# Two attention heads at a time in a one-layer hybrid decoder with a mixture of experts

## The chip, the cores and the metric

The kernel runs on one core of a Trainium2 chip. The metric is the device time of one execution in microseconds; a lower time is better. The core has engines that work side by side, each with its own in-order queue: PE (matrix multiply; PEld is its weight load), DVE (elementwise work on vectors), ACT (functions of one argument, from tables), and SP, which here only issues transfers. PSUM is the small memory that PE writes and DVE and ACT read, in eight banks of 512 float32 columns for each of 128 partitions.

## What is computed

One layer of a decoder trunk for 256 tokens of 1024 channels in float32. A vector c gives six adaLN vectors (shift, scale, gate, twice). Three causal branches (forgetting attention A, stick-breaking attention B, with 8 heads of 64 each, and a gated linear recurrence C) are projected, gated, summed and projected again; a top-4-of-32 mixture of experts follows.

```python
def token_mixer(h, ...):
    z = h @ w_in
    qa, ka, va, fa, qb, kb, vb, xc, gc = jnp.split(z, IN_SPLITS, axis=-1)
    logf = jax.nn.log_sigmoid(fa + b_f)
    o_a = fox_attention(fox_h(qa), fox_h(ka), fox_h(va), logf)
    o_b = stick_breaking_attention(sb_h(qb), sb_h(kb), sb_h(vb))
    o_c = rg_lru_branch(xc, gc, conv_w, conv_b, lru_wa, lru_ba, lru_wx, lru_bx, lru_lambda)
    g = jax.nn.sigmoid(h @ w_gate + b_gate).reshape(b, s, N_BRANCHES, d)
    merged = g[:, :, 0] * (o_a @ w_pa) + g[:, :, 1] * (o_b @ w_pb) + g[:, :, 2] * (o_c @ w_pc)
    return merged @ w_o
...
# fox_attention:   s = q k * scale + F_q - F_k, masked;  p = softmax(s);  out = p @ v
# stick-breaking:  log_keep = log_sigmoid(-z) below the diagonal;  cs = cumsum(log_keep)
#                  w = exp(log_sigmoid(z) + min(cs[-1] - cs, 0));  out = w @ v
# rg_lru:          a = exp(log_a);  u = sqrt(-expm1(2 * log_a)) * (i_gate * x)
#                  h_t = a_t * h_(t-1) + u_t;  out = h * gelu(gc)
...
ada = cond @ w_ada + b_ada            # shift1, scale1, gate1, shift2, scale2, gate2
y = token_mixer(x * (1 + scale1) + shift1, ...)
x = layer_norm(ALPHA * x + (1 + gate1) * y)
y = moe_ffn(x * (1 + scale2) + shift2, ...)
x = layer_norm(ALPHA * x + (1 + gate2) * y)
```

## The kernel before, in words

**Projections.** Weights arrive in pieces of 1 MB ([128, 2048] float32) in a ring of five buffers (`load`, L74). `split` (L90) makes a high part on ACT (L96) and a low part on DVE (L97) into one of three weight buffers; a projection is the sum of three products, 48 matmuls of 256 columns for each piece (`proj_T`, L278). Results go to PSUM tag `g`, two banks, and from there through ACT or DVE.

**Order.** The program is written in one order, and a planner then orders each engine's queue by the written order and by what it holds to be ready, so projections fill PE's queue between steps of the attention. The written order is: q, k, v of branch A in six projections (`qkv`), with the forget gates (`forget`), pairs 0 and 1 of the heads after three of them and pairs 2 and 3 after six; the same for branch B; four convolution projections (`conv`); the recurrence's gates, its roots (`Sqrt`, L521) and scans (L525); `w_pa`; the recurrence's other input `gl` (L548 to L552); gelu (L557), product (L558) and split of the recurrence's output; the first branch's gates (`gate_pair`, L569); then, for the second and third branch, gates and projections (`add_branch`, L583); then `w_o` in eight units with the routing (`unit`, `route`).

**Heads.** `fox` (L348) and `stick` (L437) take one head: scores on half of PE's rows into one bank of PSUM tag `a` (two banks), steps on DVE and ACT in one half of the SBUF tiles `da` and `db`, then transposes or a running sum into one bank of tag `b` (two banks). `attend` (L375) multiplies by the values, on half of PE's columns, into a bank `o` that the two heads of a pair share; L430 and L471 read it.

**Tables.** ACT holds one set of functions at a time. Order edges (`after`, L69: order only, no wait) keep the root behind the recurrence's exponentials (`end_exp`), the gelu and all gates' `Tanh` behind the roots (`end_sqrt`).

**The adaLN vectors.** Vectors 0 and 1 come first, on PE. The other four are summed by DVE while other work runs: `ada_rest` (L255) is a generator, and `ada_step` (L271), called after each projection, takes its next step where the string `ADA` has a 1. A vector has four loads of 1 MB, each with two multiply-adds over 1024 columns (L173, L175), and a fifth step that sums over partitions on PE and adds the bias. Before, vector 5 is summed at steps 4 to 8, vector 4 at 18 to 23, vector 3 at 24 to 29, vector 2 at 31 to 36; steps 1 to 12 are the attention's projections, 13 to 16 the convolution, 17 and 18 `w_pa`, 19 to 22 `gl`, 23 to 26 the first gates, 27 to 40 the other two branches.

**Experts.** The second part streams 2 MB chunks through eight places (`place_of`, L753) in the order `ROUND`. The places lie over memory of the first part: place 0 over the pool `low`, 1 to 3 over the ring and two slots of `mid`, 4 over the rest of `mid`, 5 to 7 over the weight buffers. So the first chunks, which SP issues in order, wait until those buffers are free.

Of the kernel before, what the change touches and what calls it, by code (L numbers as in the profile page):

```python
# [26 lines left out]
GSLOT = 6  # L27
# [3 lines left out]
ADA = "00001" "1" "111000" "0000" "00" "1111" "0111" "01110111" "1111111111"  # L31
WFAT = 1
ROUND = (0, 1, 3, 2, 5, 7, 4, 6)
# [15 lines left out]
def hybrid_layer_kernel(ctx: ExitStack, tc: tile.TileContext, a: dict, dbg=None):  # L49
# [66 lines left out]
    bank = banks(ps1, {"g": 2, "a": 2, "b": 2, "m": 2})  # L116
# [65 lines left out]
    xT = [bank("ab"[b // 2], f"xT{b}") for b in range(4)]  # L182
# [165 lines left out]
    def fox(h, qa, ka):  # L348
        hs = slice(64 * (h % 2), 64 * (h % 2) + 64)
        ft = h // 2  # L350
        p = bank("a", "fs")
        nf = negid[hs, h:h + 1].to_broadcast([64, 128])
        mm(p[:, :128], qa[hs, ft, :128], ka[hs, ft, :128], True, False)
        mm(p[:, :128], nf, FS[hs, :128], False, True)
        mm(p[:, 128:384], qa[hs, ft, 128:], ka[hs, ft, :], True, False)
        mm(p[:, 128:384], nf, FS[hs, :], False, True)
        s = da[:, h % 2, :384]
        V.scalar_tensor_tensor(s[:, :128], p[:, :128], Fq[:, 0, h:h + 1], fmask[:, 128:], op0=OP.add, op1=OP.add)
        V.scalar_tensor_tensor(s[:, 128:384], p[:, 128:384], Fq[:, 1, h:h + 1], fmask, op0=OP.add, op1=OP.add)
        st = m1.tile([128, 8], F32, tag="st", name="st", bufs=4)  # L360
        V.reduce_max(st[:, 0:1], s[:, :128], axis=AX.X, negate=True)
        V.reduce_max(st[:, 1:2], s[:, 128:384], axis=AX.X, negate=True)
        S.activation(s[:, :128], s[:, :128], AF.Exp, bias=st[:, 0:1], accum_out=st[:, 2:3])
        S.activation(s[:, 128:384], s[:, 128:384], AF.Exp, bias=st[:, 1:2], accum_out=st[:, 3:4])
        V.reciprocal(st[:, 4:6], st[:, 2:4])
        V.tensor_scalar(s[:, :128], s[:, :128], st[:, 4:5], None, op0=OP.mult)
        V.tensor_scalar(s[:, 128:384], s[:, 128:384], st[:, 5:6], None, op0=OP.mult)
        pt = bank("b", "fpt")
        for j in range(3):
            PE.transpose(pt[:, j * 128:(j + 1) * 128], s[:, j * 128:(j + 1) * 128], ident)  # L370
        w = db[:, h % 2, :384]
        S.activation(w, pt[:, :384], AF.Copy)
        return w

    def attend(h, w, v, o):  # L375

        hs = slice(64 * (h % 2), 64 * (h % 2) + 64)
        c = slice(64 * h, 64 * h + 64)
        mm(o[hs, :T], v[:, 0, c], w[:, :256], True, False)
        mm(o[hs, 128:T], v[:, 1, c], w[:, 256:384], False, True)  # L380
# [39 lines left out]
    for i, done in enumerate(qkv(0, "a", (2, 3, 4), ada_step)):  # L420
        if i == WFAT:
            FS, Fq, negid = forget()
        if done is None:
            continue
        qa, ka, va = done
        for hp in (2 * (i // 3), 2 * (i // 3) + 1):
            o = bank("m", "oa")
            for h in (2 * hp, 2 * hp + 1):
                attend(h, fox(h, qa, ka), va, o)
            S.activation(oah[:, hp, :], o[:, :T], AF.Copy)  # L430
            V.tensor_tensor(oal[:, hp, :], o[:, :T], oah[:, hp, :].bitcast(F32), op=OP.subtract)
# [5 lines left out]
    def stick(h, qb, kb):  # L437
        hs = slice(64 * (h % 2), 64 * (h % 2) + 64)
        ft = h // 2
        p = bank("a", "bs")  # L440
        mm(p[:, :256], kb[hs, ft, :128], qb[hs, ft, :], True, True)
        mm(p[:, 256:384], kb[hs, ft, 128:], qb[hs, ft, 128:], True, True)
        n = slice(0, 384)
        l = da[:, h % 2, n]
        S.activation(l, p[:, n], AF.Abs)
        S.activation(l, l, AF.Exp, scale=-1.0)
        S.activation(l, l, AF.Ln, bias=1.0)
        k = db[:, h % 2, n]
        V.scalar_tensor_tensor(k, p[:, n], 0.0, l, op0=OP.max, op1=OP.add)
        V.scalar_tensor_tensor(l, p[:, n], 0.0, l, op0=OP.min, op1=OP.subtract)  # L450
        for d in (0, 256):
            V.tensor_tensor(k[:, d:d + 128], k[:, d:d + 128], SU, op=OP.mult)
        q = bank("b", "bc")
        mm(q[:, n], SL, k, True, False)
        mm(q[:, 128:256], ones, k[:, 256:384], False, True)
        V.scalar_tensor_tensor(l, q[:, n], 0.0, l, op0=OP.max, op1=OP.subtract)
        i = S.activation(l, l, AF.Exp, scale=-1.0)
        for d in (0, 256):
            V.tensor_tensor(l[:, d:d + 128], l[:, d:d + 128], SU, op=OP.mult)
        return l, i  # L460

    for i, done in enumerate(qkv(6, "b", (7, 8, 9), ada_step)):
        if done is None:
            continue
        qb, kb, vb = done
        for hp in (2 * (i // 3), 2 * (i // 3) + 1):
            o = bank("m", "ob")
            for h in (2 * hp, 2 * hp + 1):
                w, last = stick(h, qb, kb)
                attend(h, w, vb, o)  # L470
            S.activation(obh[:, hp, :], o[:, :T], AF.Copy)  # L471
            V.tensor_tensor(obl[:, hp, :], o[:, :T], obh[:, hp, :].bitcast(F32), op=OP.subtract)
# [29 lines left out]
    for q in range(2):  # L502
        r, i, th = (f4(s, n) for s, n in zip(((7, 8, 9), (0, 1, 17))[q], ("r", "i", "th")))
        lru.append((r, i, th))
        for u in range(2):
            pr, pi = bank("a", "pr"), bank("b", "pi")
# [10 lines left out]
    for q, (r, i, th) in enumerate(lru):  # L517

        S.activation(xv[q], r, AF.Square)
        V.scalar_tensor_tensor(th, xv[q], 1.0, th, op0=OP.add, op1=OP.mult)  # L520
        end_sqrt = after(S.activation(th, th, AF.Sqrt, scale=0.25), end_exp)  # L521
        V.tensor_tensor(i, i, th, op=OP.mult)
        for f in range(4):
            c = slice(f * T, f * T + T)
            V.tensor_tensor_scan(th[:, c], r[:, c], i[:, c], 0.0, OP.mult, OP.add)  # L525

# [28 lines left out]
    oc = []  # L555
# [9 lines left out]
    tgu = f4(18, "tgu").rearrange("p (b c) -> p b c", b=2)  # L565

    last_tanh = [None]

    def gate_pair(b, i, out):  # L569

        p = proj_pair(a["w_gate"][4 * b + i])
        for f in range(2):
            c = 8 * b + 2 * i + f
            last_tanh[0] = after(S.activation(out[:, f, :], p[:, f * T:(f + 1) * T], AF.Tanh, scale=0.5,
                                              bias=hbg[:, c:c + 1]), end_sqrt)
        ada_step()

    for i in range(4):
        t = tgu[:, i % 2].rearrange("p (f t) -> p f t", f=2)
        gate_pair(0, i, t)  # L580
        V.scalar_tensor_tensor(merged(2 * i), t, 1.0, merged(2 * i), op0=OP.add, op1=OP.mult)

# [84 lines left out]
    def unit(t, j):  # L667
# [14 lines left out]
        pT = bank("a", "pT")  # L682
# [5 lines left out]
    def route(t):  # L688
        pl = bank("b", "pl")
# [569 lines left out]
```

## Time and profile before

| | us |
|---|---|
| median of 3 runs | 1318.84 (1317.68 to 1322.93) |
| profiled execution | 1319.59 |
| its span, first to last instruction | 1317.7 |
| PE busy | 1204.5 (91%) |
| DVE busy | 493.3 (37%) |
| ACT busy | 283.6 (22%) |

The mean granted clock of PE is 0.982 of full speed. Busy shares are means over stages with different limits, so the stages are read apart: the first part, up to about 376 us, has many small steps on four engines; the second, to about 1280 us, is the stream of expert weights; the last 38 us are the final norm. Ends of matmuls are modelled and rows of matmuls overlap, so a rate is best read from starts.

### The profile page before, as it was taken

How to read it: one execution, taken by the hardware profiler on the slowest of the kernel's cores; microseconds unless marked ns; L12 is line 12 of the kernel's file. 1: busy time of each engine (PE TensorE's matmuls, PEld its weight loads, DVE VectorE, ACT ScalarE, POOL GpSimd, SP SyncE). 2: the span in 40 equal slices, each digit the busy share in tenths (PEclk: the TensorE clock that was granted, in tenths of full speed). 3: DMA queues.
4: the chain of work that ended last, by engine and by line, in shares of the span. 5: the costliest groups of instructions: out<-in, count | busy, mean ns of one | idle time of the engine just before them, and what ended most of it. 6: DMA issues, size and time to landing. Idle time of an engine off the chain costs nothing. (4 is left out here: it accounts for less than half of the span.)

```text
span 1317.7 us, 15781 instructions
## 1 busy us (share of the span) xinstructions
PE 1204.5 (91%) x6508; PEld 616.8 (47%) x6508; DVE 493.3 (37%) x1018; ACT 283.6 (22%) x554; POOL 0.2 (0%) x4
## 2 busy tenths in 40 slices
PE   5899999999889999999999889979898988989895
PEld 2888899999843343433343233223223322323221
DVE  1765688977732431313122212212221221212224
ACT  1454559434220110200011010001101100101010
POOL 0000000000000000000000000000000000000000
PEclk9899999999989999999999999999999999999998
DMA  9854356794879999999999999999999999999991
GB/s 387 319 205 160 104 191 234 293 364 178 336 294 429 423 420 428 429 427 427 427 427 428 429 427 428 427 428 427 429 426 428 428 426 428 427 427 427 428 414 75
DMA packets 42771, 482.95 MB, mean 367 GB/s; under 512 B 4740, under 2 KB 5508, under 8 KB 9672
## 3 DMA queue, kind: packets, MB, share of 16 engines
q1 hardware_dynamic: 42024, 480.51, 88.1%
q10 hardware_dynamic: 672, 1.39, 0.3%
q8 instruction: 53, 0.87, 0.3%
q14 instruction: 22, 0.18, 0.0%
HBM read 480.83 MB, written 1.05 MB: 366 GB/s over the span
## 5 line engine op out<-in xcount | busy, mean ns | idle before, releaser
L64 PE MATMUL gu<-raw,xg 128*64 128x512 f32 x2048 | 460.7, 596 | 47.0 <-DMA raw<-in_w_gu_dram 46.7
L64 PEld LDWEIGHTS gu<-raw,xg 128*64 128x64 f32 x2048 | 140.0, 137 | 352.8 <-issue 264.4
L64 PE MATMUL yp<-raw,act 128*64 128x512 f32 x992 | 230.0, 605 | 6.2 <-DMA raw<-in_w_down_dram 3.7
L871 DVE TENSOR_TENSOR t<-pT,bge 128x256 f32<-128x256 f32 x128 | 48.4, 419 | 392.9 <-PE pT L865 391.6
L855 ACT ACTIVATE gs<-gu 128x512 f32<-128x512 f32 x64 | 38.1, 597 | 639.4 <-PE gu L64 593.9
L64 PE MATMUL pp<-hh,w 128*128 128x256 f32 x896 | 130.6, 291 | 4.7 <-ACT hh L104 4.7
L64 PEld LDWEIGHTS yp<-raw,act 128*64 128x64 f32 x992 | 67.7, 138 | 139.8 <-issue 123.8
L64 PEld LDWEIGHTS pp<-hh,w 128*128 128x128 f32 x896 | 116.7, 194 | 8.8 <-ACT hh L104 4.8
L97 DVE TENSOR_TENSOR w<-raw,w 128x2048 fp32r<-128x2048 f32 x44 | 100.6, 2287 | 34.6 <-ACT w L96 34.5
L96 ACT ACTIVATE w<-raw 128x2048 fp32r<-128x2048 f32 x44 | 84.0, 1911 | 28.3 <-PE pm L64 12.8
L939 DVE TENSOR_TENSOR x<-x,pC 128x512 f32<-128x512 f32 x60 | 38.7, 684 | 119.3 <-PE pC L64 119.3
L64 PE MATMUL pC<-y,G 64*128 64x512 f32 x248 | 68.0, 622 | 6.8 <-DVE y L894 6.4
L894 DVE TENSOR_TENSOR y<-yp,g2c 128x512 f32<-128x512 f32 x31 | 21.4, 691 | 136.6 <-PE yp L64 136.6
L64 PE MATMUL pp<-hl,w 128*128 128x256 f32 x448 | 66.2, 287 | 0.0
L64 PEld LDWEIGHTS pp<-hl,w 128*128 128x128 f32 x448 | 59.0, 193 | 1.0 <-issue 0.7
L874 ACT ACTIVATE sg<-t 128x256 f32<-128x256 f32 x64 | 26.7, 417 | 98.5 <-DVE t L872 98.5
L64 PEld LDWEIGHTS pC<-y,G 64*128 64x128 f32 x248 | 23.1, 185 | 49.0 <-issue 33.0
L865 PE MATMUL pT<-cst,gs 128*128 128x128 f32 x256 | 41.1, 286 | 4.5 <-ACT gs L855 3.7
L865 PEld LDWEIGHTS pT<-cst,gs 128*128 128x128 f32 x256 | 26.9, 140 | 38.8 <-ACT gs L855 30.4
L818 ACT ACTIVATE xg<-pgx 128x128 f32<-128x128 f32 x128 | 28.5, 275 | 55.7 <-PE pgx L64 54.9
L175 DVE SCALAR_TENSOR_TENSOR acc<-raw,cond,acc 128x1024 f32<-128x1024 f32 x28 | 35.9, 1281 | 3.2 <-DMA raw<-in_w_ada_dram 3.0
L64 PE MATMUL pgx<-P,h2h 128*128 128x256 f32 x128 | 31.2, 326 | 3.1 <-ACT G L834 0.9
(278 smaller groups left out, 897.5 us busy)
## 6 DMA issues: line engine op xcount, KB each, us to landing
raw<-in_w_gu_dram SPq DMA_DIRECT2D x128, 2048.0 KB, 32.7
raw<-in_w_down_dram SPq DMA_DIRECT2D x62, 2048.0 KB, 32.3
raw<-in_w_ada_dram SPq DMA_DIRECT2D x24, 1024.0 KB, 7.3
raw<-in_w_in_dram SPq DMA_DIRECT2D x20, 1024.0 KB, 7.0
raw<-in_w_gate_dram SPq DMA_DIRECT2D x12, 1024.0 KB, 7.2
raw<-in_w_pc_dram SPq DMA_DIRECT2D x4, 1024.0 KB, 8.6
raw<-in_w_o_dram SPq DMA_DIRECT2D x4, 1024.0 KB, 4.9
rawl<-in_w_down_dram SPq DMA_DIRECT2D x3, 1024.0 KB, 32.1
```

The costliest lines, as they stand in the source:

```text
L64: PE.matmul(out, lhsT, rhs, start=start, stop=stop)
L96: i = S.activation(wh[:, c], r, AF.Copy)
L97: j = V.tensor_tensor(wl[:, c], r, wh[:, c].bitcast(F32), op=OP.subtract)
L175: V.scalar_tensor_tensor(acc, raw[:, i, :], cond[:, k:k + 1], acc, op0=OP.mult, op1=OP.add)
L818: S.activation(x[:, k].rearrange("p e s -> p (e s)"), p[:, i * 2 * CAP:(i + 1) * 2 * CAP], AF.Copy)
L855: S.activation(gs[n], gu[n], AF.Copy)
L865: PE.transpose(p[:, f * 128:(f + 1) * 128], gs[n][:, f * 128:(f + 1) * 128], ident)
L871: V.tensor_tensor(t[:, i], pv[:, i], b[:, :, None].to_broadcast([128, 4, CAP]), op=OP.add)
L874: S.activation(sg, t[:, 0], AF.Sigmoid, scale=1.702)
L894: V.tensor_tensor(y, yp, g2c, op=OP.mult)
L939: V.tensor_tensor(acc[t][:, c], acc[t][:, c], p[n], op=OP.add)
```

## The change

`fox`, `stick` and `attend` take a pair of heads (`hp`). PSUM tags `a` and `b` become one tile of two banks each (`wide`), one bank for each head; steps that are alike for both heads become one instruction over both banks or over both halves of `da` and `db`, and matmuls of the two heads are written alternately. The recurrence's gate tiles `pr`, `pi` and three other users of the tags take such a tile too. The block with the recurrence's roots and scans moves behind the first branch's four gates, whose `Tanh` is now ordered behind `end_exp` alone; the roots are ordered behind the last of these, the other gates behind the gelu. `ADA` now has vector 5 at steps 4 to 8, vector 4 at 9 to 13, vector 3 at 27 to 31, vector 2 at 32 to 37; vector 4's accumulator is slot 14 instead of 6. `ROUND` swaps places 1 and 2.

```diff
-GSLOT = 6
+GSLOT = 14
...
-ADA = "00001" "1" "111000" "0000" "00" "1111" "0111" "01110111" "1111111111"
+ADA = "0000" "1111111111" "0000000000000" "11111111111111111"
...
-ROUND = (0, 1, 3, 2, 5, 7, 4, 6)
+ROUND = (0, 2, 3, 1, 5, 7, 4, 6)
...
-    bank = banks(ps1, {"g": 2, "a": 2, "b": 2, "m": 2})
+    bank = banks(ps1, {"g": 2, "m": 2})
+    def wide(tag, name):
+        return ps1.tile([128, 2, 512], F32, tag=tag, name=name)
...
+    HALF = slice(0, 64), slice(64, 128)
+    def fox(hp, qa, ka):
+        p = wide("a", "fs")
+        for c, q in ((slice(0, 128), slice(0, 128)), (slice(128, 384), slice(128, 256))):
+            k = slice(0, c.stop - c.start)
+            for i, hs in enumerate(HALF):
+                mm(p[:, i, c], qa[hs, hp, q], ka[hs, hp, k], True, False)
+            for i, hs in enumerate(HALF):
+                mm(p[:, i, c], negid[hs, 2 * hp + i:2 * hp + i + 1].to_broadcast([64, 128]), FS[hs, k], False, True)
+        s = da[:, :, :384]
...
+        for t, c in ((0, slice(0, 128)), (1, slice(128, 384))):
+            V.reduce_max(st[:, 0, 2 * t:2 * t + 2], s[:, :, c], axis=AX.X, negate=True)
...
+        pt = wide("b", "fpt")
+        for i in range(2):
+            for j in range(3):
+                PE.transpose(pt[:, i, j * 128:(j + 1) * 128], s[:, i, j * 128:(j + 1) * 128], ident)
+        w = db[:, :, :384]
+        S.activation(w, pt[:, :, :384], AF.Copy)
         return w
...
+    def attend(hp, w, v, o):
+        for t, oc, wc in ((0, slice(0, T), slice(0, 256)), (1, slice(128, T), slice(256, 384))):
+            for i, hs in enumerate(HALF):
+                c = slice(64 * (2 * hp + i), 64 * (2 * hp + i) + 64)
+                mm(o[hs, oc], v[:, t, c], w[:, i, wc], t == 0, t == 1)
...
-            for h in (2 * hp, 2 * hp + 1):
-                attend(h, fox(h, qa, ka), va, o)
+            attend(hp, fox(hp, qa, ka), va, o)
...
+    def stick(hp, qb, kb):
+        p = wide("a", "bs")
+        for c, k, q in ((slice(0, 256), slice(0, 128), slice(0, 256)),
+                        (slice(256, 384), slice(128, 256), slice(128, 256))):
+            for i, hs in enumerate(HALF):
+                mm(p[:, i, c], kb[hs, hp, k], qb[hs, hp, q], True, True)
+        p = p[:, :, n]
+        l, k = da[:, :, n], db[:, :, n]
+        S.activation(l, p, AF.Abs)
...
+        V.scalar_tensor_tensor(k, p, 0.0, l, op0=OP.max, op1=OP.add)
+        V.scalar_tensor_tensor(l, p, 0.0, l, op0=OP.min, op1=OP.subtract)
...
+        q = wide("b", "bc")
+        for i in range(2):
+            mm(q[:, i, n], SL, k[:, i, :], True, False)
+            mm(q[:, i, 128:256], ones, k[:, i, 256:384], False, True)
...
+        prw, piw = wide("a", "pr"), wide("b", "pi")
         for u in range(2):
-            pr, pi = bank("a", "pr"), bank("b", "pi")
+            pr, pi = prw[:, u, :], piw[:, u, :]
...
+    behind = [end_exp]
+    def gate_pair(b, i, out):
...
+                                              bias=hbg[:, c:c + 1]), behind[0])
...
+    for i in range(4):
+        t = tgu[:, i % 2].rearrange("p (f t) -> p f t", f=2)
+        gate_pair(0, i, t)
+        V.scalar_tensor_tensor(merged(2 * i), t, 1.0, merged(2 * i), op0=OP.add, op1=OP.mult)
+    for q, (r, i, th) in enumerate(lru):
+        after(S.activation(xv[q], r, AF.Square), end_exp)
+        V.scalar_tensor_tensor(th, xv[q], 1.0, th, op0=OP.add, op1=OP.mult)
+        end_sqrt = after(S.activation(th, th, AF.Sqrt, scale=0.25), last_tanh[0])
+        V.tensor_tensor(i, i, th, op=OP.mult)
+        for f in range(4):
+            c = slice(f * T, f * T + T)
+            V.tensor_tensor_scan(th[:, c], r[:, c], i[:, c], 0.0, OP.mult, OP.add)
...
-        after(S.activation(gl[q], gl[q], AF.Gelu_apprx_tanh), end_sqrt)
+        behind[0] = after(S.activation(gl[q], gl[q], AF.Gelu_apprx_tanh), end_sqrt)
```

## Rows read from the trace of the kernel before

**Rows 1.** Page, 40 slices: tenths of the time that DMA engines moved data.
```profile
DMA  9854356794879999999999999999999999999991
```

**Rows 2.** Stages: length, busy us of PE, PEld, DVE, ACT, POOL; clock, DMA share, GB/s.
```profile
110.00:190.00 80.00, 80.00 (x575) 71.02 (x574) 55.45 (x98) 42.32 (x63) 0.00 (x0) 1.00 0.41 144
190.00:243.00 53.00, 53.00 (x413) 50.71 (x412) 48.26 (x53) 41.67 (x58) 0.00 (x0) 1.00 0.65 230
243.00:294.20 51.20, 51.20 (x409) 49.28 (x409) 43.85 (x38) 19.81 (x20) 0.00 (x0) 1.00 0.95 369
294.20:333.00 38.80, 37.88 (x314) 37.36 (x313) 26.95 (x25) 19.26 (x18) 0.00 (x0) 1.00 0.46 167
376.00:1280.00 904.00, 834.08 (x3832) 293.36 (x3832) 213.94 (x569) 100.04 (x275) 0.00 (x0) 1.00 1.00 424
```

**Rows 3.** PE's timeline: start us, busy us, line, operation, out<-in, shape, count.
```profile
72.92 0.34 PE L64 MATMUL fs<-FS,negid 64*128 64x128 f32 x2
...
73.79 1.10 PE L64 MATMUL pp<-hh,w 128*128 128x256 f32 x7
...
105.31 2.08 PE L64 MATMUL pt<-w,hh 128*128 128x256 f32 x16
107.23 1.12 PE L64 MATMUL pt<-w,hl 128*128 128x256 f32 x8
108.28 0.88 PE L64 MATMUL oa<-d,va 128*64 128x256 f32 x8
109.09 1.21 PE L64 MATMUL pt<-w,hh 128*128 128x256 f32 x8
110.23 0.93 PE L64 MATMUL bs<-qTb,kTb 64*128 64x256 f32 x8
111.09 0.86 PE L64 MATMUL pp<-hh,w 128*128 128x256 f32 x5
...
115.29 0.86 PE L64 MATMUL oa<-d,va 128*64 128x256 f32 x4
...
120.75 0.92 PE L64 MATMUL bs<-qTb,kTb 64*128 64x256 f32 x4
```

**Rows 4.** PE's waits for other engines, 38 to 358 us: total us, times, longest.
```profile
PE pp L64 <- ACT hh L104: 4.7, 1, 4.7
PE py L64 <- ACT mh L104: 0.9, 1, 0.9
```

**Rows 5.** Stages by tile, PE first: `fs`, then `oa`, `bs`, `ob`.
```profile
50.00:212.00 162.00, 7.17 (x48) 4.92 (x48) 5.99 (x16) 1.00 0.54 192
50.00:212.00 162.00, 6.06 (x32) 3.30 (x32) 1.67 (x4) 1.53 (x4) 1.00 0.54 192
50.00:212.00 162.00, 6.43 (x32) 4.72 (x32) 8.73 (x16) 3.97 (x8) 1.00 0.54 192
50.00:212.00 162.00, 5.43 (x32) 2.79 (x32) 1.67 (x4) 1.52 (x4) 1.00 0.54 192
```

**Rows 6.** DVE, groups by line, 40 to 380 us: count, busy us, mean ns, idle.
```profile
L175 DVE SCALAR_TENSOR_TENSOR acc<-raw,cond,acc 128x1024 f32<-128x1024 f32 x28 | 35.9, 1281 | 3.2 <-DMA raw<-in_w_ada_dram 3.0
...
L525 DVE TENSOR_TENSOR_SCAN th<-r,i 128x256 f32<-128x256 f32 x8 | 4.9, 670 | 0.0
...
L522 DVE TENSOR_TENSOR i<-i,th 128x1024 f32<-128x1024 f32 x2 | 2.4, 1216 | 0.0
```

**Rows 7.** ACT's timeline, the table for the roots and the two gelus.
```profile
214.72 1.28 ACT L521 ACT_TABLE_LOAD   x1
...
222.08 2.00 ACT L557 ACTIVATE gl<-gl 128x1024 f32<-128x1024 f32 x2
```

**Rows 8.** SP's timeline: transfers of the first expert chunks, issue times.
```profile
311.54 56.74 SPq L759 DMA_DIRECT2D raw<-in_w_gu_dram  x8
...
333.74 0.93 SPq L759 DMA_DIRECT2D raw<-in_w_gu_dram  x2
```

**Rows 9.** ACT's timeline, a stick pair's first step, in brackets its wait.
```profile
130.44 0.49 ACT L445 ACTIVATE d<-bs 128x384 f32<-128x384 f32 x1 [2.60 <-PE ob L64]
```

More of the change, by code (lines that the diff above doesn't have):

```diff
@@ L179, in col_sums @@
         mm(p, acc[:, h * 128:(h + 1) * 128], ones[:, 0:1], True, True)
-    xT = [bank("ab"[b // 2], f"xT{b}") for b in range(4)]
+    xT = [w[:, i, :] for w in (wide("a", "xTa"), wide("b", "xTb")) for i in range(2)]
     for b in range(4):
@@ L346, in hybrid_layer_kernel @@
     oah, oal = (four(f4(i, n, F32R)) for i, n in ((5, "oah"), (6, "oal")))
[L348 to L372, printed above, removed]
-        return w
@@ L375, in attend @@
[L375 to L380, printed above, removed]
+    HALF = slice(0, 64), slice(64, 128)
[8 more added lines that the diff above has]
+        s = da[:, :, :384]
+        st = m1.tile([128, 3, 4], F32, tag="st", name="st", bufs=3)
+        blocks = [(t, c, i) for t, c in ((0, slice(0, 128)), (1, slice(128, 384))) for i in range(2)]
+        for t, c, i in blocks:
+            V.scalar_tensor_tensor(s[:, i, c], p[:, i, c], Fq[:, t, 2 * hp + i:2 * hp + i + 1],
+                                   fmask[:, 128:] if t == 0 else fmask, op0=OP.add, op1=OP.add)
+        for t, c in ((0, slice(0, 128)), (1, slice(128, 384))):
+            V.reduce_max(st[:, 0, 2 * t:2 * t + 2], s[:, :, c], axis=AX.X, negate=True)
+        for t, c, i in blocks:
+            n = 2 * t + i
+            S.activation(s[:, i, c], s[:, i, c], AF.Exp, bias=st[:, 0, n:n + 1], accum_out=st[:, 1, n:n + 1])
+        V.reciprocal(st[:, 2, :], st[:, 1, :])
+        for t, c, i in blocks:
+            n = 2 * t + i
+            V.tensor_scalar(s[:, i, c], s[:, i, c], st[:, 2, n:n + 1], None, op0=OP.mult)
+        pt = wide("b", "fpt")
[4 more added lines that the diff above has]
+        S.activation(w, pt[:, :, :384], AF.Copy)
+        return w
@@ L467, in hybrid_layer_kernel @@
             o = bank("m", "ob")
-            for h in (2 * hp, 2 * hp + 1):
-                w, last = stick(h, qb, kb)
-                attend(h, w, vb, o)
+            w, last = stick(hp, qb, kb)
+            attend(hp, w, vb, o)
             S.activation(obh[:, hp, :], o[:, :T], AF.Copy)
@@ L516, in hybrid_layer_kernel @@
         V.scalar_tensor_tensor(i, i, 1.0, xv[q], op0=OP.add, op1=OP.mult)
[L517 to L525, printed above, removed]
     mg = [four(f4(2 + q, f"merged{q}")) for q in range(2)]
@@ L552, in hybrid_layer_kernel @@
         ada_step()
+    tgu = f4(18, "tgu").rearrange("p (b c) -> p b c", b=2)
+    last_tanh = [None]
+    behind = [end_exp]
+    def gate_pair(b, i, out):
+        p = proj_pair(a["w_gate"][4 * b + i])
+        for f in range(2):
+            c = 8 * b + 2 * i + f
+            last_tanh[0] = after(S.activation(out[:, f, :], p[:, f * T:(f + 1) * T], AF.Tanh, scale=0.5,
+                                              bias=hbg[:, c:c + 1]), behind[0])
+        ada_step()
+    for i in range(4):
[10 more added lines that the diff above has]
+            V.tensor_tensor_scan(th[:, c], r[:, c], i[:, c], 0.0, OP.mult, OP.add)
     oc = []
     for q, (r, i, th) in enumerate(lru):
-        after(S.activation(gl[q], gl[q], AF.Gelu_apprx_tanh), end_sqrt)
+        behind[0] = after(S.activation(gl[q], gl[q], AF.Gelu_apprx_tanh), end_sqrt)
         V.tensor_tensor(th, th, gl[q], op=OP.mult)
@@ L562, in hybrid_layer_kernel @@
     dump("oc", oc[0][0].bitcast(F32))
[L565 to L581, printed above, removed]
     def add_branch(b, x, src, nk):
@@ L681, in unit @@
         V.bn_stats(stats[t][:, j, :], xs[t][:, c])
-        pT = bank("a", "pT")
+        pT = wide("a", "pT")[:, 0, :]
         for i in range(2):
@@ L688, in route @@
     def route(t):
-        pl = bank("b", "pl")
+        pl = wide("b", "pl")[:, 0, :]
         for k in range(8):
```

21 lines of the change are left out of this document (4 added, 17 removed).

## Prediction

> **What bounds the kernel now.** I read the slices of the page first, then the busy time by stage, then PE's waits. The DMA digits [rows 1] split the run: from the thirteenth slice on (395 us) the engines that move data are full, before it they are not. The windows [rows 2] say it with numbers: from 376 to 1280 us the DMA share is 1.00 at 424 GB/s, while PE is busy 834 of 904 us. The expert stage runs at the speed of its weight stream. Nothing in the diff changes the bytes of that stage, so I count it as a block of fixed length that begins when the first part is over. In the first part PE is busy in every microsecond from 110 to 294 us [rows 2]. As ends of matmuls are modelled, I checked this with starts: 16 projection matmuls took 1.92 us (105.31 to 107.23), 120 ns each [rows 3], and from 243 to 294.2 us 409 were started, 125 ns each, wider ones included [rows 2]. Between 38 and 358 us PE waited for another engine 4.7 us at the very start and 0.9 us at the end [rows 4]. So PE's own matmul time is the bound: what the change takes from PE there should come off the total nearly one for one, and what it takes from DVE or ACT is worth nothing by itself.
>
> **The change, part by part.** *Heads in pairs.* A head uses half of PE's rows (scores) or half of its columns (values). Where both heads of a pair were queued alternately, they already overlap: the eight score matmuls of a stick pair at 110.23 are busy 0.93 us, the four of one head at 120.75 0.92 us; the eight value matmuls of a pair at 108.28 take 0.88 us, the four of one head at 115.29 0.86 us [rows 3]. So a pair costs what one head costs. Before, they mostly weren't together: of 7 runs of stick scores 1 is a pair, of 7 of forget values 1, of 7 of stick values 2. The new code makes both heads ready in the same instant: both score products wait for one PSUM tile, both value products for one copy (L372) or one mask step (L459). With every pair joined, from the busy totals [rows 5]: stick scores 6.43 - 4 x 0.93 = 2.7 us, forget values 6.06 - 4 x 0.88 = 2.5, stick values 5.43 - 4 x 0.88 = 1.9. A joined pair's later forget scores take 0.87 us from 72.92 to the next projection at 73.79 [rows 3]; with the part before I estimate 1.3 a pair, so 7.17 - 4 x 1.3 = 2.0. Together 9.1 us. A busy row reaches 0.07 us into the next (108.28 + 0.88 against 109.09), so for some 11 runs saved I take off 0.8: **8.3 us**. The transposes (L370) and the running sum (L454) use the full array and keep their time.
>
> *Fewer breaks.* Changing between projection and attention costs PE on both sides: the 8 projection matmuls between values and scores take 1.14 us (109.09 to 110.23), the 8 before the values 1.05 us (107.23 to 108.28), against 0.96 at 120 ns [rows 3]. So a break costs some 0.18 us besides its own matmuls. In that view I count about 50 breaks between 57 and 212 us, the recurrence's gate products included; joined pairs and gate tiles of two banks should leave 35 to 44. That is 1 to 3 us; I take **2 us**.
>
> *DVE and ACT in the attention.* Wider instructions save a little of both, and the summed adaLN vector adds to DVE eight products over 1024 columns, 8 x 1.28 = 10.2 us [rows 6], between 110 and 190 us, where DVE is busy 55.5 of 80 us [rows 2]. It fits; without that cover it would cost up to 10 us. Its four loads of 1 MB pass SP in a stretch at 144 GB/s [rows 2]. Its accumulator takes slot 14, so `wab`, which is loaded into that slot, can go out on SP only after the vector's sums are read, one convolution projection after the attention's; three more projections and the first of `w_pa` stand between that and its use. PE's matmuls for the vector move and don't change. Price 0, at most 1 us.
>
> *Roots behind the first gates.* On ACT the first gates no longer wait for two table loads of 1.28 us, two roots and two gelus, which ended at 224 us [rows 7]; PE lost nothing there, so this gains 0. Now the same chain, 2 x 1.28 + 2 x 1.05 + 2.0 = 6.7 us (a root takes about half of the gelu row's 2.0), or 8.6 with one weight split between, stands before the second branch's gates. PE has two banks for projections, 2 x 48 matmuls = 11.5 us of work, before it needs the first of these gates' banks again. Price 0; bound 2 us.
> On DVE the second products, scans, gelu products and splits (2.4 + 4.9 + 2.4 + 2.4 = 12.1 us; [rows 6] has the first two, the others are as wide as the first) move into the stretch 243 to 294 us, where DVE is busy 43.9 of 51.2 us [rows 2]. Three instructions of the next adaLN vector come in and some of the last one go out, about -1 us. That makes 55 us of work in 51.2 us. In the stretch after it DVE is busy 27.0 of 38.8 us [rows 2], so 4 us of adaLN sums can flow over. I price it at **+1 us**, bounds 0 and 6.5 (4 us of overflow and 5% of idling between dependent steps).
>
> *Order of the first weight chunks.* They go out between 311.5 and 368 us, the second and third together at 333.74 [rows 8]; the list swaps the second and the fourth place. Were the place that it now wants second free only when the last of `w_o` is split, some 8 us later (about 341), three chunks would leave together there, and at 4.9 us a chunk (2 MB at 428 GB/s) the eighth would land near 376 us, as the expert stage begins. PE needs 3.4 us for each chunk, so hardly one is late. Price 0, bounds -1 and +2.
>
> **Sum:** -8.3 - 2 + 1 + 0.3 for the rest = **-9 us**, against the profiled execution's 1319.59 us (span 1317.7, 1.9 us around it): 1310.6. The median of the runs is 0.75 us lower, which gives 1309.8; I say **1310**.
>
> **Rivals.**
> *(1) DVE becomes the bound.* If DVE can't carry the overflow above, or the roots' chain is late, PE waits up to 6.5 us between 250 and 295 us, and a gain of 2 to 6 remains: 1313 to 1317. For it: DVE at 86% there before, and full after. Against it: from 190 to 243 us DVE was busy 48.3 of 53 us [rows 2] and PE lost nothing. In the Trainium skill, "TensorEngine Tiling (Array Packing)", the section on the PSUM bottleneck says that packing speeds up PE but not the emptying of PSUM, which may then become the bound. By that rule this rival would win already in the attention; there the trace speaks against it, as DVE has a third of its time free from 110 to 190 us [rows 2].
> *(2) The heads stay apart.* The planner that orders PE's queue may put projections between the heads as before. Then only merged DVE and ACT work is left, which is hidden: -1 to -3 us, 1316 to 1318. Against it: where both heads were ready at once, they were queued alternately.
> *(3) Slower: a pair is one chain.* Before, head 0 could run its exponentials while head 1 was scored. Now each step waits for both heads, and the score tile and the transposes' tile exist once. If PE's in-order queue reaches a pair's sums or values before they are ready, all projections behind them wait. The nearest row is the 2.6 us that ACT waited for a pair's last values before the next pair's absolute values [rows 9]. Were such a wait exposed on PE in each of eight pairs, it would cost 21 us: 1319 - 10 + 21 = 1330. It decides from 1.3 us a pair on (10.3 us by 8). Against it: pairs already went one after the other, through the same `da` and `db`, as that very row shows, and PE did not wait.
>
> **How the numbers follow.** Forecast, 1305 to 1312: 0.60. Rival 1, 1312 to 1317: 0.18. Rival 2, with small losses on top, 1316 to 1321: 0.12. Rival 3, 1322 to 1335: 0.10. The low end takes all bounds in favour: -8.3 - 3 - 1 - 0.9 (the wait of [rows 4]) = -13.2, 1305.6; I go 1 us lower for what a new order of PE's queue may bring. The range 1304.5 to 1319 leaves out rival 3 and part of rival 2, less than 2 in 10. A measurement of this kernel tells about 0.5%, 6.6 us, from no change, so faster means under 1312.2: 0.62. Within: 0.29. Slower, over 1325.4: 0.09.
>
> **What would show it.** Stick scores and both kinds of values in four runs of eight matmuls each, about 0.9 us busy; fewer breaks; projections at 120 ns up to the routing; the first expert matmul near 367 us instead of 376, and the rest of the trace as long as before. PE idle before a gate or a projected branch between 250 and 295 us would show rival 1; single-head runs rival 2; PE waiting for `d` between 75 and 200 us rival 3. Wrong altogether would be a first expert matmul at 367 us and an end that did not move: then something before the first part's end bounds the stream.

## The result and the profile after

The changed kernel took 1327.38 us (median of 4 runs, 1326.99 to 1328.43) against 1320.12 us for the kernel before on the same chip (4 runs): ratio 1.0059, 95% interval 1.0043 to 1.0075. It is slower by some 7 us, where 10 us less were forecast. The profiled execution spans 1325.5 us.

Pairing did on PE what it should. The first fence is PE's timeline of the changed kernel (start, duration, operation, count), the rows that answer to [rows 3].

```profile
116.82 0.87 PE L64 MATMUL oa<-d,va 128*64 128x256 f32 x8
...
150.09 0.92 PE L64 MATMUL bs<-qTb,kTb 64*128 64x256 f32 x8
...
161.22 0.87 PE L64 MATMUL ob<-d,vb 128*64 128x256 f32 x8
...
201.63 0.87 PE L64 MATMUL ob<-d,vb 128*64 128x256 f32 x8
...
384.33 1.51 PE L64 MATMUL gu<-raw,xg 128*64 128x512 f32 x6
```

Eight matmuls of two heads take 0.87 or 0.92 us; forget and stick values stand in four such runs each, stick scores in five. Counted from start to start, scores and values take 15.0 us of PE instead of 23.1. Yet the last pair's values come at 201.6 us, where before they came at 195.8, and the first expert matmul at 384.33 us, where before it came at 375.98. From there on the kernel takes as long as before (941.2 and 941.7 us), so the loss lies ahead of it. PE's waits from 38 to 358 us (us in total, times, longest) were 0.9 us before, but for the start [rows 4]. Now, besides the start and 1.1 us at the end, they are:

```profile
PE pr L64 <- ACT r L524: 4.3, 5, 1.5
PE pp L64 <- DVE tgu L606: 3.0, 1, 3.0
PE pp L64 <- ACT tgu L567: 2.7, 1, 2.7
PE pm L64 <- DVE w L97: 1.2, 1, 1.2
```

The windows say in which stretch. The rows that answer to [rows 2], columns as there:

```profile
110.00:190.00 80.00, 79.92 (x631) 73.51 (x630) 58.12 (x84) 45.56 (x56) 0.00 (x0) 1.00 0.41 142
190.00:243.00 53.00, 45.78 (x304) 39.88 (x303) 22.09 (x23) 30.99 (x48) 0.00 (x0) 0.90 0.32 110
243.00:294.20 51.20, 46.97 (x369) 45.55 (x368) 47.28 (x44) 25.51 (x26) 0.00 (x0) 0.97 0.67 247
```

Up to 190 us PE starts 631 matmuls instead of 575: it is ahead. From 190 to 243 us it starts 304 instead of 413. There the recurrence's gates, on which the tanh of the first branch's gates waits, are late. The load of `wab` on SP's queue, and PE as the recurrence runs (the bracket is the idle time before a row and what ended it):

```profile
210.61 0.33 SPq L83 DMA_DIRECT2D wab<-in_wab_dram  x1
```

```profile
226.74 1.22 PE L64 MATMUL pr<-xv,wab 128*128 128x256 f32 x2 [0.64 <-ACT r L524]
228.53 1.22 PE L64 MATMUL pr<-xv,wab 128*128 128x256 f32 x2 [0.56 <-ACT r L524]
232.49 2.08 PE L64 MATMUL pp<-hh,w 128*128 128x256 f32 x8 [2.74 <-ACT tgu L567]
234.37 1.91 PE L64 MATMUL pp<-hl,w 128*128 128x256 f32 x8
236.08 2.40 PE L64 MATMUL pp<-hh,w 128*128 128x256 f32 x16
```

`wab` goes out 102 us later than before (108.78). The vector whose accumulator sits in its slot is summed on PE only behind the attention's last values, at 202.43 us and 207.76 us. So from 219 us on nothing but the recurrence's gate products is left for PE, and five times it waits for a tanh (L524). After the last wait eight matmuls take 1.88 us from start to start (232.49 to 234.37) instead of 0.96.

This table sets the runs side by side; each column is one instruction of the profiled execution (us), the waits are those of PE for other engines from 60 to 300 us.

| kernel | ratio to before (95%) | `wab` issued | last `ob` | recurrence's last exp ends | first gate's tanh | PE's waits | first expert matmul |
|---|---|---|---|---|---|---|---|
| before | 1 | 108.8 | 196.4 | 214.7 | 224.0 | 0 | 376.0 |
| after | 1.0059 (1.0043 to 1.0075) | 210.6 | 202.2 | 231.7 | 231.6 | 11.2 | 384.3 |
| old_round | 1.0072 (1.0055 to 1.0089) | 210.6 | 202.2 | 232.6 | 232.5 | 11.0 | 385.1 |
| old_sums | 1.0030 (1.0015 to 1.0045) | 105.2 | 206.0 | 228.5 | 228.4 | 8.8 | 381.5 |
| sums_earlier | 1.0031 (1.0016 to 1.0047) | 169.8 | 207.7 | 228.1 | 228.0 | 8.5 | 381.7 |
| pairs_only | 1.0040 (1.0027 to 1.0052) | 104.1 | 204.9 | 227.4 | 236.4 | 13.5 | 382.0 |
| sums_only | 1.0083 (1.0059 to 1.0107) | 208.5 | 203.7 | 232.5 | 241.8 | 7.6 | 389.8 |
| sums_early_only | 1.0046 (1.0029 to 1.0063) | 170.7 | 201.9 | 219.5 | 236.0 | 2.7 | 382.7 |
| roots_only | 1.0039 (1.0026 to 1.0053) | 107.9 | 195.5 | 212.8 | 221.5 | 4.3 | 381.3 |
| lockstep | 0.9996 (0.9986 to 1.0007) | 108.6 | 196.7 | 213.9 | 230.4 | 0 | 376.5 |
| joined_narrow | 0.9940 (0.9923 to 0.9957) | 106.6 | 188.8 | 204.8 | 221.4 | 0 | 367.5 |
| wide_tiles | 1.0134 (1.0109 to 1.0159) | 103.9 | 221.0 | 235.8 | 244.8 | 14.1 | 390.3 |
| joined_rest | 1.0088 (1.0071 to 1.0105) | 214.8 | 205.1 | 233.2 | 233.1 | 12.7 | 386.5 |

### The profile page after: what moved, and what is told of

Same layout as the page of the kernel before. It is cut to its first block, busy times and chain, and to the rows that moved or that the text cites. A ratio compares the mean times of both kernels' runs of the same rounds, so it can differ in the third digit from the quotient of the medians.

```text
span 1325.5 us, 15733 instructions
## 1 busy us (share of the span) xinstructions
PE 1199.3 (90%) x6508; PEld 616.0 (46%) x6508; DVE 492.1 (37%) x978; ACT 284.7 (21%) x534; POOL 0.2 (0%) x4
## 5 line engine op out<-in xcount | busy, mean ns | idle before, releaser
L97 DVE TENSOR_TENSOR w<-raw,w 128x2048 fp32r<-128x2048 f32 x44 | 100.8, 2290 | 31.4 <-ACT w L96 31.3
```

The lines of the kernel that those rows point to most:

```text
L97: j = V.tensor_tensor(wl[:, c], r, wh[:, c].bitcast(F32), op=OP.subtract)
```

## The experiments

The first theories, as the expectations name them: **S**, the sums in slot 14 hold back `wab`; **R**, the new place of the roots costs; **P**, a pair is one chain and delays attention and recurrence. Later **C** stands for P with its cause: two heads share one PSUM tile and its wide steps; its rival **M** says that matmuls of two heads that wait for one another are enough.

### Undoing one part: the sums

`old_sums` is the changed kernel with the sums of before; `sums_earlier` is it with the new sums one step earlier.

```diff
 old_sums
-GSLOT = 14
+GSLOT = 6
-ADA = "0000" "1111111111" "0000000000000" "11111111111111111"
+ADA = "00001" "1" "111000" "0000" "00" "1111" "0111" "01110111" "1111111111"
 sums_earlier
-ADA = "0000" "1111111111" "0000000000000" "11111111111111111"
+ADA = "000" "1111111111" "00000000000000" "11111111111111111"
```

> The changed kernel with one part undone: the steps of the adaLN sums (ADA) and the accumulator's slot are those of the kernel before; pairs, roots behind the gates and the order of places stay. Theory S (the sums): vector 4's accumulator holds slot 14 until PE sums it behind the last stick pair, so wab is loaded at 210.6 us, the recurrence's gates come late, and PE idles some 13 us between 219 and 232 us; then this kernel loads wab near 109 us, that hole is gone, and so is part of the 4 us lost near 260 us: 1310 to 1314 us, 13 to 17 below the changed kernel and 6 to 10 below the one before. Theory R (the roots): the first gates' functions, now in front of the roots but behind the recurrence's exponentials, fill both projection banks; then the hole stays, 1325 to 1328. Theory P (the pairs): one chain for two heads delays the recurrence; the hole stays too.

> The changed kernel with the steps of vectors 5 and 4 each one step earlier (3 to 12 instead of 4 to 13), so the sums of vector 4 are written ahead of the last two stick pairs, in the same slot 14. Theory S, in the form that the slot is held by sums queued behind the attention's last outputs: the sums come 20 us or more earlier, wab is loaded by about 190 us, the hole of 13 us between 219 and 232 us shrinks to under 4: 1314 to 1319 us. Theories R and P: no change, 1326 to 1329. If only the share of DVE matters and not the slot: no change either.

Both stand at 1.003, where S had forecast a time under that of before. Some of the loss goes when `wab` goes out early, whether the vector is summed during the attention or not: 3.8 us by the ratios, whose intervals overlap a little with that of the changed kernel, and 2.6 to 2.8 us by the first expert matmul. So in the changed kernel the late `wab` is worth some 3 to 4 us, and S is part of the cause, not all of it.

### Doing one part alone

`pairs_only` is the kernel before with the change's heads, attention and gate tiles; `sums_only` has only the new `ADA` and `GSLOT`; `roots_only` only the moved roots with their order edges.

```diff
 pairs_only
-    bank = banks(ps1, {"g": 2, "a": 2, "b": 2, "m": 2})
+    bank = banks(ps1, {"g": 2, "m": 2})
...
 sums_only
-GSLOT = 6
+GSLOT = 14
...
 roots_only
+        end_sqrt = after(S.activation(th, th, AF.Sqrt, scale=0.25), last_tanh[0])
...
```

> The kernel before with the pairs alone (two heads at a time, PSUM tiles of two banks, gate tiles of two banks); sums, roots and places as before. Theories S and R: PE saves 8 us in the attention, as its rows in the changed kernel show (23.1 to 15.0 us of steps), and some breaks, and nothing gives it back: 1309 to 1313. Theory P: the hole is here too, 1322 to 1330.

> The kernel before with the new steps of the adaLN sums and slot 14 alone; heads one at a time, roots in their old place, old order of places. Theory S: wab waits for the sums here as well and is loaded about 100 us later than in the kernel before; the recurrence is late, and with the roots ahead of the gates the hole is as large or larger: 1328 to 1340. Theories R and P: 1318 to 1322, as before.

> The kernel before with only the recurrence's roots and scans moved behind the first gates. Theory C: before has no idle PE at the first gates, so nothing can be gained; the later scans and splits cost as much as they do with pairs, 4 to 5 us at 250 to 268 us: ratio 1.003 to 1.004. Rival: that hole comes only because the attention ends late, and here it doesn't: ratio 0.999 to 1.001.

Each part alone is slower: 5.3, 10.8 and 5.4 us by the medians beside them.

`pairs_only` was a miss for S and R. PE does 7.1 us less for scores and values, and then idles 13.5 us. Its rows of ACT, then of PE:

```profile
197.28 0.82 ACT L469 ACTIVATE d<-d 128x768 f32<-128x768 f32 x1
198.12 1.28 ACT L524 ACT_TABLE_LOAD   x1
...
226.78 0.60 ACT L527 ACTIVATE r<-r,cn 128x256 f32<-128x256 f32 x1
227.39 1.28 ACT L533 ACT_TABLE_LOAD   x1
...
236.45 1.55 ACT L586 ACTIVATE tgu<-pp,hbg 128x256 f32<-128x256 f32 x4
```

```profile
225.05 0.70 PE L64 MATMUL pi<-xv,wxb 128*128 128x256 f32 x2 [1.90 <-ACT i L525]
237.32 2.08 PE L64 MATMUL pp<-hh,w 128*128 128x256 f32 x8 [11.58 <-ACT tgu L586]
```

The last exponential of the attention runs at 197.28 us (190.15 before), the table load for the recurrence follows it, the root's table comes at 227.39 us (214.72 [rows 7]), and the first gates' tanh at 236.45 us (223.99). Chain by chain: 7.1 us later out of the attention, 5.5 us more in the recurrence, -0.2 in the roots, 12.5 together. Before, PE ended the second gate piece and began the third at about 231.6 us (ACT's second tanh waits for it until 231.63), while the first tanh had freed a bank at 224.8: the chain had 7 us to spare. PE, its waits apart, arrives some 8 us earlier and the tanh comes 12.5 later, so it waits 8 + 12.5 - 7 = 13.5 us, as measured (1.90 + 11.58). Part of the 5.5 us may lie in the recurrence's gate tiles, which this kernel also widens; no run takes them apart.

`roots_only` shows a second place, with PE, SP and ACT, DVE and the granted clock (the eighth column of the windows):

```profile
255.97 1.22 PE L64 MATMUL pm<-obh,w 128*128 128x256 f32 x8 [1.22 <-DVE w L97]
...
264.15 2.07 PE L64 MATMUL pp<-hh,w 128*128 128x256 f32 x8 [3.12 <-ACT w L96]
266.03 1.69 PE L64 MATMUL pp<-hl,w 128*128 128x256 f32 x8
```

```profile
255.94 4.46 SPq L78 DMA_DIRECT2D raw<-in_w_gate_dram  x2
...
262.19 1.91 ACT L96 ACTIVATE w<-raw 128x2048 fp32r<-128x2048 f32 x1 [3.38 <-DMA raw<-in_w_gate_dram]
```

```profile
247.84 4.76 DVE L573 TENSOR_TENSOR_SCAN th<-r,i 128x256 f32<-128x256 f32 x8
252.52 1.20 DVE L578 TENSOR_TENSOR th<-th,gl 128x1024 f32<-128x1024 f32 x1
253.63 2.29 DVE L97 TENSOR_TENSOR w<-raw,w 128x2048 fp32r<-128x2048 f32 x1
255.84 0.75 DVE L173 TENSOR_SCALAR acc<-raw,cond 128x1024 f32<-128x1024 f32 x1
```

```profile
264.15:267.50 3.35, 3.35 (x16) 3.35 (x17) 3.35 (x3) 1.91 (x1) 0.00 (x0) 0.53 0.10 22
267.60:272.00 4.40, 4.40 (x39) 4.40 (x39) 4.37 (x5) 0.00 (x0) 0.00 (x0) 1.00 0.86 315
```

DVE runs scans and products without a pause from 245.6 us on. The weight's low part (L97) queues behind them, and PE waits 1.2 us for it. It is also the last reader of a ring buffer: as it ends, at 255.92 us, SP issues the load of the next gate's weight (255.94; before, the load that stands there went out at 245.03). ACT's split waits 3.4 us for that load and PE 3.1 us for the split. The second load of that row goes out at 260.07, as an adaLN product (L175) ends at 260.05. From 200 to 300 us ACT waits 10.3 us for weights, 7.7 before. After that PE runs at half its clock for 3.4 us. Waits of 4.3 us and some 1.4 us of slow matmuls come to 5.7, near the 5.3 us by which the first expert matmul is late. This is rival 1's place, and it needs neither pairs nor sums.

### The sums alone, with `wab` early

```diff
-GSLOT = 6
+GSLOT = 14
-ADA = "00001" "1" "111000" "0000" "00" "1111" "0111" "01110111" "1111111111"
+ADA = "000" "1111111111" "00000000000000" "11111111111111111"
```

> The kernel before with vectors 5 and 4 summed at steps 3 to 12 and slot 14 for vector 4's accumulator, one step earlier than in the change; chunk order, heads and roots as before. With the change's own steps (the sums alone) wab went out at 208 us and the kernel lost 10.9 us. If wab's late load is the whole cost, it goes out before 175 us here and the time is that of before: ratio 0.999 to 1.002. If DVE's eight products in the attention cost as well, the last ob is late (200 us or more against 196) and ratio 1.003 to 1.007.

5.5 us remain of 10.8. The late `wab` is about half of what the sums cost alone. In the rest PE waits only 2.7 us; its scores and values take 24.9 us instead of 23.1, in more runs of one head (11 of stick scores, 9 of stick values; 7 and 7 before), and the last values come 5.5 us later. DVE's busy time was not it: from 110 to 190 us it is 54.1 us here and 55.5 before. What differs is the order in the queues: ACT takes the first step of the first stick pair at 118.2 us instead of 113.0. That the vector's steps stand ahead of the heads' on DVE fits this, and wasn't tried apart.

### Free banks for the gates

If PE only waits for banks that hold gate sums, copying them out should end the wait. `pairs_copy` and `old_sums_copy` add this to `pairs_only` and `old_sums`; `pairs_copy2` also orders the roots behind the recurrence's last tanh.

```diff
         p = proj_pair(a["w_gate"][4 * b + i])
+        V.tensor_copy(out, p.rearrange("p (f t) -> p f t", f=2))
...
-            last_tanh[0] = after(S.activation(out[:, f, :], p[:, f * T:(f + 1) * T], AF.Tanh, scale=0.5,
+            last_tanh[0] = after(S.activation(out[:, f, :], out[:, f, :], AF.Tanh, scale=0.5,
```

> Pairs alone (roots, sums and chunk order as before), and every gate's sum is copied out of PSUM by DVE at once, its tanh then works in SBUF. Theory C says that PE's idle 12 us at 225 to 237 us are a wait for the two banks that the first gates' tanh hold, and nothing else: with the banks free PE goes on for two more pieces, the first expert matmul comes 8 to 12 us earlier than the 382 us of pairs alone, and the time is 6 to 10 us under before: ratio 0.992 to 0.996. If another thing held PE there (the weights' split, DVE), at most 4 us come back: ratio 1.000 to 1.003.

> Pairs alone with the gates' sums copied out of PSUM by DVE, and the roots ordered behind all of the recurrence's tanh, so that no root stands between two of them. With the copies alone the table went to the root, back to tanh and to the root again, and the first gates' tanh came at 243.4 us against 236.4 in pairs alone, while PE idled 14 us behind the two SBUF places of the copies. If the wait is only for places held by late gates, these tanh now come near 238 us, PE's idle time falls to 4 to 8 us, ratio 1.000 to 1.003. If it stays at 12 us or more, ratio 1.004 or above, the tanh that come late aren't a matter of the roots' order.

> The changed kernel with the sums of before (vector 4 in slot 6), and every gate's sum copied out of PSUM by DVE. Without the copies PE is idle 5 us at 223 to 229 and 5 us at 254 to 264 us. Theory C: both are waits for banks that gates hold, so both go, ratio 0.993 to 0.997. Rival 1 of the prediction (DVE is the bound from 243 us on): the first hole goes, the second stays or grows by the copies, ratio 0.998 to 1.001.

All three missed: 1.0069 (1.0051 to 1.0087), 1.0075 (1.0053 to 1.0097) and 1.0030 (1.0020 to 1.0040). PE's row in `pairs_copy2`:

```profile
249.89 2.05 PE L64 MATMUL pp<-hh,w 128*128 128x256 f32 x8 [14.26 <-DVE tgu L584]
```

The wait began at 235.6 us instead of 225.7, so the copies bought 10 us of cover. But it ended 12.6 us later: the first tanh came at 243.4 us instead of 236.4, the second root alone waits 4.3 us for DVE, behind scans and a split, and a freed place now passes through DVE's queue as well. With the roots ordered the wait stayed as long as in `pairs_copy` (14.0 us), so the order of the roots wasn't what made the tanh late. The edit changed the chain that it should have uncovered, so it doesn't tell the size of the wait. That the wait is one for held places, both rows show. In `old_sums_copy` PE has no wait before 247 us, so the first hole is gone, as both theories had it; from 247 to 278 us it waits 8.2 us, for weights' splits, so the second stays, as rival 1 had it.

### One tile for two heads, or a bank for each

Four kernels take the pair apart. `lockstep`: the kernel before, matmuls of two heads written alternately, all else for each head alone. `joined_narrow`: the same, and order edges hold the matmuls of the two heads together. `wide_tiles`: `pairs_only` with narrow steps, the two-bank tile kept; from `lockstep` it differs in the tiles alone, those of the recurrence's gates among them. `pairs_only` has the tile and wide steps.

```diff
 lockstep
-        p = bank("a", "bs")
+        ps = [bank("a", "bs") for _ in HALF]
...
+            for p, hs in zip(ps, HALF):
+                mm(p[:, c], kb[hs, hp, k], qb[hs, hp, q], True, True)
 joined_narrow, on top: stick scores behind the last pair's sums, head 0's values behind head 1's
+                i = mm(p[:, c], kb[hs, hp, k], qb[hs, hp, q], True, True)
+                if sums[0]:
+                    after(i, sums[0])
...
+            for i, hs in reversed([*enumerate(HALF)]):
...
+                first = after(j, first) if first else j
 wide_tiles
+        pa, pb = wide("a", "bs"), wide("b", "bc")
+        ps = [pa[:, i, :] for i in range(2)]
```

> The kernel before, with only the written order of a pair changed: the score matmuls and the value matmuls of the two heads are written alternately, but each head keeps its own PSUM bank and its own narrow steps on DVE and ACT. Theory C (the wide steps make a pair one chain; the attention ends later though PE does less, and the time saved on PE is lost again at the first gates): the heads' chains stay staggered, the last ob stays near 196 to 199 us, no hole on PE at 220 to 237 us, and most of the pairing's 8 us is gained: 5 to 8 us under before, ratio 0.994 to 0.996. Rival M (to let the matmuls of two heads wait for one another is enough to delay the attention): a hole before the first gates as in the kernel with pairs alone, ratio 1.000 to 1.004.

> The kernel before, with the two heads' score and value matmuls written alternately and held together by order edges on PE (a pair's value matmuls start with the head that is ready last; the next pair's stick scores stand behind both running sums), but with one PSUM bank and narrow steps for each head as before. In PE's planned queue all score and value runs are then pairs of heads, and the last of the attention stands 19.4 projections from the start, as in before (19.3; 22.3 in pairs alone). Theory C (the pairs' wide tile and wide steps make one chain of two heads, and what that delays eats the gain): here PE saves 6 to 8 us, the attention ends at 188 to 198 us, the first gates cost PE nothing, the first expert matmul comes at 368 to 371 us and the time is 5 to 8 us under before, ratio 0.994 to 0.996. Rival M (the end of the attention and the recurrence are a chain that PE's work doesn't set at all): PE saves the time and idles it away before the first gates, ratio 0.998 to 1.002.

> Pairs alone, with the two-bank tiles kept, but every step on DVE and ACT done for each head by itself as before. In PE's planned queue the attention ends later still, 24.0 projections from the start against 22.3 with wide steps and 19.3 in before. If the wide steps are what delays the pairs, this lies between before and pairs alone: ratio 1.000 to 1.003. If the shared tile is (a tile is handed on as a whole, so the second head's steps queue behind the first's), it is slower than pairs alone: last ob at 212 to 220 us, ratio 1.006 to 1.015.

`lockstep` neither gained nor lost, where C had forecast 5 to 8 us less: the second head is ready a little later than the first (ACT's first steps stand 0.7 us apart in before, at 174.9 and 175.6), and projections still go between them (stick scores in 7 runs, as before). `joined_narrow` has stick scores and both kinds of values in four runs of pairs each (forget scores in seven), on PE:

```profile
107.81 0.92 PE L64 MATMUL bs<-qTb,kTb 64*128 64x256 f32 x8
...
127.32 0.87 PE L64 MATMUL ob<-d,vb 128*64 128x256 f32 x8
...
188.18 0.87 PE L64 MATMUL ob<-d,vb 128*64 128x256 f32 x8
...
367.45 3.65 PE L64 MATMUL gu<-raw,xg 128*64 128x512 f32 x16
```

```profile
190.00:243.00 53.00, 53.00 (x421) 51.56 (x420) 45.73 (x46) 40.59 (x53) 0.00 (x0) 1.00 0.62 227
```

Scores and values take 16.3 us, the attention ends 7.6 us earlier than before, PE is busy throughout, and the first expert matmul stands at 367.45 us. The median is 1310.46 us (6 runs) against 1318.96: **faster by 8.5 us**, or 0.4 to 0.8%. This version beats both kernels, and M falls. `wide_tiles` is the slowest of all (1335.67 us). Its ACT rows show the first steps of the two heads of a pair, with DVE's last step on the first head's scores between them:

```profile
144.78 0.47 ACT L458 ACTIVATE d<-bs 128x384 f32<-128x384 f32 x1
...
148.51 0.55 DVE L462 SCALAR_TENSOR_TENSOR d<-bs,d 128x384 f32<-128x384 f32 x1
...
151.51 0.47 ACT L458 ACTIVATE d<-bs 128x384 f32<-128x384 f32 x1
```

The second head's first step comes 6.7 us after the first head's; in `joined_narrow` 0.6 us (145.2 and 145.8). So with a bank for each head the attention isn't late, in two kernels, and with one tile it is, in two. The wide steps are not what delays it: without them the shared tile costs 11 us more (16.7 and 5.3 against before). In each of the four stick pairs of `wide_tiles` the second head's first step waits for DVE and starts only after that last step on the first head's scores has ended, 3.7 to 9.3 us behind the first head's (0.6 or 0.7 us in `joined_narrow`). That fits a tile that is handed on as a whole. What the gate tiles add is open.

### The rest of the change, and the chunk order

`joined_rest` puts the change's sums, roots and chunk order on `joined_narrow`; `joined_round` only the chunk order; `old_round` is the changed kernel with the order of before.

```diff
-ROUND = (0, 1, 3, 2, 5, 7, 4, 6)
+ROUND = (0, 2, 3, 1, 5, 7, 4, 6)
```

> The whole change (sums, slot 14, roots behind the first gates, chunk order), except that its pairs are those of the kernel with joined heads, with a PSUM bank and narrow steps for each head. If the parts only add, it stands at -8.5 + 10.9 + 5.4 = +8 us: ratio 1.006. If the late recurrence that the sums bring hides the roots' cost, as in the changed kernel, ratio 1.001 to 1.004. If the shared tile was all that was wrong with the change, ratio 0.993 to 0.997.

> The kernel with joined heads and the change's order of the first chunks. Priced at 0, bounds -1 and +2: ratio 0.993 to 0.996, as without it (0.994).

> The changed kernel with the chunk order of before. The prediction priced the swap of two places at 0, bounds -1 and +2: the same as the changed kernel, ratio 1.004 to 1.007 to before. If the new order was worth something, 1.007 to 1.010.

`joined_rest` took 1331.21 us, 1.0088 (1.0071 to 1.0105): `wab` at 214.8 us, the last values at 205.1, PE's waits 12.7 us. With the change's sums and roots the new pairs lose all they had gained and end 12.1 us over before, more than the sum of the parts (+8 us, 1.006). They are no faster there than the change's own pairs (1.0059): beside those sums and roots, a bank for each head wins nothing back. Why is open. `joined_round` stands at 0.9938 (0.9921 to 0.9955) and `old_round` at 1.0072: the swap is worth nothing that can be told.

## Why the prediction was wrong

The step that failed is the first: from "PE's own matmul time is the bound" it took that PE's saving comes off the total "nearly one for one", and from "PE did not wait" that a pair's longer chain, the late `wab` and the moved scans cost next to nothing. The saving came, and from 60 to 300 us PE waited 11.2 us where it had waited for nothing.

*What bounds the kernel.* "PE's own matmul time is the bound" was right for the kernel before, and `joined_narrow` shows it: scores and values took 6.7 us less of PE, projections 2.5 less, all else 0.7 more, and the first expert matmul came 8.5 us earlier; the median fell by as much. (That it stands at 367.45 us where 367 was forecast is partly luck: the forecast had 10.3 us for the pairs and 1.3 against them for parts that this kernel hasn't.) What the step left out is how near the next bound lay. The chain from the attention's last exponential through the recurrence to the first gates' tanh had 7 us to spare before; a look at the first gate bank, free at 224.8 us and needed at 231.6, would have given it.

*Pairs.* The term was right: -8.3 forecast, -8.1 measured in the changed kernel, -6.7 in `joined_narrow`, where forget scores gained 0.1. Breaks fell from 50 to 37 (41 in `joined_narrow`, whose projections took 2.5 us less, near the 2 forecast). Before, the first projection matmul behind a run on half the array took 222 to 253 ns on the mean of each tile, against 121 in the rest. The Trainium skill, "TensorEngine Tiling (Array Packing)", section "Tiling Modes", under "Key Properties", says that a change of tiling mode drains TensorE. The trace can't tell such a cost apart: behind the transposes, which use the full array, that matmul took 201 ns. Rival 1's rule from the same page of the Trainium skill, that emptying PSUM becomes the bound, did not come true in the attention: DVE is busy 58.1 of 80 us from 110 to 190 us.

*Rival 3* named the right mechanism, a pair as one chain, and the wrong place. No projection waited for a pair's sums or values in the changed kernel; that 1327 us falls into this rival's 1322 to 1335 is luck. The row against it, pairs that went one after the other through `da` and `db` [rows 9], was read as if nothing could get longer. It did: with the change's pairs the attention ended 6 to 11 us later instead of earlier, and the price came behind it, as 13.5 us up to the first gates in `pairs_only`. "PE did not wait" says nothing about a chain as long as there is other work to put between; each pair's longer way let PE run through that work earlier, and it was missing later.

*The vector in slot 14* was priced at 0, at most 1 us. Its cover was counted in the written order ("one convolution projection after the attention's"), but the sum on PE came behind the attention's last values in the queue and `wab` at 210.6 us. In the changed kernel that is some 3 to 4 us, alone with the rest of the sums 10.8. That the products "fit" beside DVE's other work was right by busy time, and still the sums cost 5.5 us with `wab` early.

*Roots.* "Price 0; bound 2 us" on ACT was right: in `roots_only` PE never waits for a tanh. On DVE +1 us was forecast, bounds 0 and 6.5: 5.4 us measured alone. The overflow went where rival 1 put it, 250 to 268 us; the step that failed was to count DVE's work by stage and let it "flow over", though DVE's queue also holds the low parts and adaLN products that give back the ring buffers of the next weights.

*Order of the chunks.* Price 0, within the bounds.

The forecast put +1.3 us against -10.3. Measured alone, roots, sums and the pair's tiles cost 5.4, 10.8 and 13.8 (5.3 + 8.5, the gate tiles among them); less the gain of 8.5 that would be 21.5, and 7 us were measured. One reason stands in the table: before, 9.3 us of tables, roots and gelu lie between the recurrence's last exponential and the first gate's tanh; with the roots moved it follows at once (231.7 and 231.6). So the move that costs 4.2 us of waits from 258 to 268 us in the changed kernel takes 9 us out of the chain that sums and pairs delay, and `old_sums`, pairs with moved roots, is no slower than `pairs_only` (1324.41 and 1326.47 us). In the changed kernel the starts on PE close the account from 38 us to the first expert matmul: scores and values -8.1 us, projections with the waits behind them +6.0, the recurrence's gate products with theirs +10.7, all else -0.2, together +8.4. How much of the +10.7 each part would have brought by itself stays open.

## What to carry to other kernels

Before work is taken from a busy engine, measure the slack of the longest dependent chain beside it: the time between a buffer's release and its next use tells how much of the gain can come through. Give each of two independent chains its own buffer, and join them only where they must be joined, with an order edge; one tile for both can cost more than the joined instructions save. Here that paid only with the sums and the roots left as they were. When an accumulator borrows a slot, look at where in the engine's queue its last reader stands, not where it was written.

## What was not expected of the hardware

A wait on PE cost more than its own length. After 3.1 us of idling in `roots_only` the granted clock was 0.50 of full speed from 264.15 to 266.20 us, 0.53 over the whole 3.35 us shown above, and then 1.00; 13 matmuls ran at 213 ns instead of 120. In the changed kernel 30 did, in all some 3 us, after its two longest waits. The Trainium skill, "TensorE: Matmul & The Clock Gate", Part 1, gives 1.2 GHz for an idle TensorE and 2.4 GHz for a busy one; the trace agrees, with 0.50 and 1.00. A sum that prices an idle stretch should add it.
